# Softmax over 32,768 columns on one Trainium2 core: part of two stores cut into transfers of a few partitions

## Chip, core and metric

One core of a Trainium2 chip runs the kernel. The metric is device time in microseconds (us), the median of several runs; less is better. Besides the compute engines, the core has 16 DMA engines, which carry out all transfers between the chip's main memory (HBM) and its on-chip memory (SBUF, 128 partitions). A transfer is issued by one of the engines SP, ACT or GpSimd (POOL), each through its own queue, and ends by raising a semaphore by 16, on which others wait.

## What is computed

```python
logits = np.random.randn(16, 256, 32768).astype(np.float32)   # temperature = 1.0
scaled = logits / temperature
scaled = scaled - scaled.max(axis=-1, keepdims=True)
exp_scaled = np.exp(scaled)
return exp_scaled / exp_scaled.sum(axis=-1, keepdims=True)
```

A softmax over each of 4096 rows of 32,768 float32: 537 MB are read and as many written.

## The kernel before

Each row is cut in two halves of 16,384 columns, so that there are 8192 half rows; 128 of them, one per partition, make a chunk, and there are G = 64 chunks. Two neighbouring partitions hold the halves of one row. A chunk is handled in two column pieces (c = 0 and 1) of `_CW` = 8192 columns, 32 KB per partition and 4 MB in all. SBUF holds six such pieces, the slots of the tensor `xs` (`X` in the code); chunk g uses slots 2g mod 6 and the next, so three chunks are in work at a time.

For a chunk, VectorE takes the maximum of each piece (L123), ScalarE (ACT) replaces the piece by its exponentials and sums them (L168), VectorE combines the pieces and the two halves of each row by a few operations on 128 x 4 numbers (L134 to L153), and then scales both pieces (L157). Results lie in the slots where the logits were. The scaling of piece k raises the semaphore `sc` k of its chunk, for which the store waits.

The order of each queue is written out by hand:

- SP issues the loads. The first chunk's two pieces are loaded in two transfers of 4096 columns each (`load_edge`, L98), the next two chunks' whole (`load`, L90). Then a loop of 20 turns loads three chunks per turn: for each of the six slots it waits until the slot's last store has landed (`st[b]`) and issues the load. After the loop come the loads of the last chunk, in four transfers.
- ACT issues the stores (`store`, L103) of chunks 0 to 60, each right behind its own work on that chunk: those of chunk 0 ahead of its loop, the others within it.
- SP issues the stores of the last three chunks, G-3, G-2 and G-1, after its loads: two transfers for each of the first two, four for G-1. At the end SP waits until every slot's stores have landed.
- GpSimd takes no part, but for four small memsets at the start.

`Half` is the class that holds the work of a chunk; its method `stores` waits for each piece's `sc` and issues its store. `first()`, `turn(q, i)` and `last(g)` make such objects for chunk 0, for those of the loop and for the last three. The semaphores `ld` and `st` have one for each slot, and are never set back: a wait asks for 16 times the number of transfers so far.

## Time and profile before

| | |
|---|---|
| median of 3 runs | 2488.28 us (2488.11 to 2488.37) |
| the profiled execution | 2488.27 us, its span 2486.5 us |
| moved | 1073.77 MB, 432 GB/s over the span |
| VectorE busy | 1724.6 us (69%) |
| ScalarE busy | 944.5 us (38%) |
| GpSimd busy | 0.2 us, 4 instructions |
| a load of 4 MB | 26.5 us from issue to landing (median) |
| a store of 4 MB by ACT | 48.3 us from issue to landing (median) |
| a store of 4 MB by SP | 33.7 us from issue to landing (median) |

The span runs from the first instruction to the last. The profile's page divides it into 40 slices; in the row of the DMA engines, a digit is the mean busy share of all 16 in tenths, 9 for 90% and more. Queue q1 holds the transfers that SP issues, q10 those of ACT, q14 the fetches of instructions. In a timeline, a line begins with the start and the time taken, then the engine (SPq and ACTq are the parts of SP and ACT that issue transfers), the line of the kernel, the operation and what it writes from what. In the table of windows the columns are named in its first line. The trace also has a record of every packet of the DMA engines (start, time taken, size, queue, but not the engine) and of each of the 16 raises of a transfer's semaphore, its landings.

### The profile page before, as it was taken

To read this page: it belongs to the slowest core of one execution; us is meant where nothing else is said; L and a number is where in the kernel's file an instruction comes from. 1 tells how busy PE (TensorE), PEld (TensorE's weight loads), DVE (VectorE), ACT (ScalarE), POOL (GpSimd) and SP (SyncE) were. 2 spreads that over 40 slices of the span, in tenths; PEclk is the share of its full clock that TensorE was granted. 3 is DMA by queue.
4 is the path that set the end of the run, shared out by engine and by line. 5 is a ranking of instruction groups with operands and counts; after the bars stand their busy time and mean duration, and the time that the engine had idled before them with its cause. 6 is when DMAs were issued, how large, how long until landed. Compare 5 with 4: busy or idle time off the path is not lost.

```text
span 2486.5 us, 2019 instructions
## 1 busy us (share of the span) xinstructions
DVE 1724.6 (69%) x644; ACT 944.5 (38%) x325; POOL 0.2 (0%) x4
## 2 busy tenths in 40 slices
DVE  6777767767677676676766767667676676766764
ACT  3444333343333433434334343343433434334342
POOL 0000000000000000000000000000000000000000
DMA  9999999999999999999999999999999999999999
GB/s 413 430 435 433 430 438 431 430 438 431 432 436 431 436 432 431 438 430 432 437 430 434 435 430 438 431 430 438 431 432 436 431 436 432 431 438 431 430 437 399
DMA packets 37730, 1073.77 MB, mean 432 GB/s; under 512 B 4192, under 2 KB 4192, under 8 KB 4192
## 3 DMA queue, kind: packets, MB, share of 16 engines
q1 hardware_dynamic: 20160, 562.05, 52.4%
q10 hardware_dynamic: 17568, 511.71, 47.7%
q14 instruction: 2, 0.02, 0.0%
HBM read 536.87 MB, written 536.87 MB: 432 GB/s over the span
## 4 chain that ended last, share of the span: by engine, by line
DMA 58%; DVE 18%; another core or an unknown queue 14%; ACT 8%; issue 1%; SPq 0%; ACTq 0%; DVEq 0%
DMA out_dram<-xs 37%; DMA xs<-in_logits_dram 21%; DVE t L123 11%; ACT xs L168 7%; DVE xs L157 6%; SPq L90 0%; ACT ee L179 0%; DVE t L134 0%; DVE row L153 0%; DVE row L138 0%; DVE junk L142 0%; ACTq L103 0%; SPq L98 0%; DVEq L133 0%
## 5 line engine op out<-in xcount | busy, mean ns | idle before, releaser
L168 ACT ACTIVATE xs<-xs,t 128x8192 f32<-128x8192 f32 (+1 forms) x130 | 912.1, 7016 | 1468.4 <-DVE t L123 1468.4
L123 DVE TENSOR_REDUCE t<-xs 128x1 f32<-128x8192 f32 (+1 forms) x130 | 1110.8, 8551 | 234.0 <-DMA xs<-in_logits_dram 234.0
L157 DVE TENSOR_SCALAR xs<-xs,ee,row 128x8192 f32<-128x8192 f32 (+1 forms) x130 | 576.5, 4478 | 2.3
L134 DVE LOAD_MASK_SELECT t<-t x64 | 0.9, 14 | 470.3 <-ACT xs L168 470.3
L179 ACT ACTIVATE ee<-t,row 128x4 f32<-128x4 f32 x64 | 19.0, 298 | 35.9 <-DVE row L138 35.9
L142 DVE CUSTOM_DVE_ANT_1 junk<-ee,t 128x4 f32<-128x4 f32 x64 | 10.4, 163 | 23.3 <-ACT ee L179 23.3
L168 ACT ACTIVATION_READ_ACCUMULATOR xs<-xs,t 128x1 f32 x130 | 24.3, 187 | 0.0
L153 DVE RECIPROCAL row<-row 128x1 f32<-128x1 f32 x64 | 10.5, 164 | 2.2
L138 DVE TENSOR_REDUCE row<-t 128x1 f32<-128x4 f32 x64 | 10.1, 157 | 2.2
L134 DVE STREAM_SHUFFLE t<-t 128x4 f32<-128x4 f32 x64 | 10.2, 160 | 0.6
L142 DVE DVE_READ_ACCUMULATOR2_ANT row<- 128x1 f32 x64 | 5.3, 82 | 0.0
L168 ACT ACT_TABLE_LOAD x1 | 1.3, 1283 | 0.9 <-SPq L54 0.9
L272 POOL MEMSET const-bfloat16-1.0<- 128x1 bf16 x1 | 0.1, 102 | 0.0
L272 POOL MEMSET const-uint8-127<- 128x1 uint8 x1 | 0.1, 101 | 0.0
L272 POOL MEMSET const-float32-0.0<- 128x1 f32 x1 | 0.1, 99 | 0.2 <-issue 0.2
L272 POOL MEMSET const-float32-1.0<- 128x1 f32 x1 | 0.1, 98 | 0.0
## 6 DMA issues: line engine op xcount, KB each, us to landing
xs<-in_logits_dram SPq DMA_DIRECT2D x124, 4096.0 KB, 26.5
out_dram<-xs ACTq DMA_DIRECT2D x122, 4096.0 KB, 48.3
xs<-in_logits_dram SPq DMA_DIRECT2D x8, 2048.0 KB, 16.1
out_dram<-xs SPq DMA_DIRECT2D x4, 4096.0 KB, 33.7
out_dram<-xs SPq DMA_DIRECT2D x4, 2048.0 KB, 21.9
```

Source lines behind the costliest of these rows:

```text
L123: m = dve.tensor_reduce(out=t[:, k : k + 1], in_=xcols(self.slots[c], s, w), axis=X_, op=A.max, negate=True)
L134: dve.stream_shuffle(out=t[:, 2 * K : 4 * K], in_=t[:, 0 : 2 * K], mask=swap).then_inc(site(tag, "sh"), 1)
L138: dve.tensor_reduce(out=r[:, 0:1], in_=tv[:, :, 0, :], axis=XY, op=A.min).then_inc(site(tag, "mx"), 1)
L142: dve.tensor_tensor_reduce(out=j[:, 0 : 2 * K].rearrange("p (a k) -> p a k", a=2), in0=e[:, 0 : 2 * K].rearrange("p (a k) -> p a k", a=2), ...
L153: dve.reciprocal(out=r[:, 2:3], in_=r[:, 1:2]).then_inc(site(tag, "rc"), 1)
L157: dve.tensor_scalar(out=xs, in0=xs, scalar1=e[:, k : k + 1], scalar2=r[:, 2:3], op0=A.mult, op1=A.mult).then_inc(site(tag, "sc", k), 1)
L168: a = act.activation(out=xs, in_=xs, func=Exp, bias=t[:, k : k + 1], scale=inv_t, accum_out=t[:, K + k : K + k + 1],)
L179: act.activation(out=e[:, 0 : 2 * K].rearrange("p (a k) -> p a k", a=2), in_=tv[:, :, 0, :], func=Exp, bias=r[:, 0:1], scale=-1.0,).then_i ...
L272: nc = _bacc.Bacc("TRN2", target_bir_lowering=False, num_devices=1)
```

## The change

Two stores are cut.

Chunk 0, first piece: ACT stores the first 6144 of its 8192 columns as before. The last 2048 columns are stored by GpSimd, which waits for the same semaphore, in transfers of 15 partitions: eight of them, and a ninth of 8. They raise a semaphore `pool` of their own. SP waits for all nine after the first six pieces are loaded, ahead of its loop, since the loop's first load overwrites that slot.

Chunk G-2 (62 of 0 to 63), first piece: SP stores the first 6400 columns as before. The last 1792 follow in 29 transfers, issued by SP one after the other: 7, 6, 5, 4, 3, 2 and 1 partitions, four times over, which makes 112 partitions, and one of 16. They raise a semaphore `stair`, for which SP waits at the end. The chunk's second piece is stored after them.

```diff
+_TURNCOLS = 2048
+_STAIRCOLS = 1792
...
+    n_pool = -(-P // 15)
+    sp.wait_ge(site("pool"), 16 * n_pool)
     with sp.Fori(1, turns + 1) as i:
...
     f = first()
     f.scalar()
-    f.stores(act, 0)
+    cut = _CW - _TURNCOLS
+    act.wait_ge(site(f.tag, "sc", 0), 1)
+    store(act, 0, 0, 0, 0, cut)
+    act.wait_ge(site(f.tag, "sc", 1), 1)
+    store(act, 0, 1, 1, 0, _CW)
+
+    pool = nc.gpsimd
+    pool.wait_ge(site(f.tag, "sc", 0), 1)
+    for p in range(0, P, 15):
+        n = min(15, P - p)
+        pool.dma_start(out=o[bass.ds(p, n), cut:_CW], in_=X[p : p + n, cut:_CW]).then_inc(site("pool"), 16)
...
+    n_stair = 0
     for g in range(G - 3, G):
-        last(g).stores(sp, g)
+        h = last(g)
+        if g != G - 2:
+            h.stores(sp, g)
+            continue
+
+        b, keep = h.slots[0], _CW - _STAIRCOLS
+        sp.wait_ge(site(h.tag, "sc", 0), 1)
+        store(sp, g, 0, b, 0, keep)
+        p = 0
+        while p < P:
+            for n in [7, 6, 5, 4, 3, 2, 1] if p < 112 else [16]:
+                sp.dma_start(
+                    out=o[bass.ds(g * P + p, n), keep:_CW],
+                    in_=X[p : p + n, b * _CW + keep : (b + 1) * _CW],
+                ).then_inc(site("stair"), 16)
+                n_stair += 1
+                p += n
+        sp.wait_ge(site(h.tag, "sc", 1), 1)
+        store(sp, g, 1, h.slots[1], 0, _CW)
+    sp.wait_ge(site("stair"), 16 * n_stair)
```

## Prediction

> **What bounds the kernel now.** I read the slices of the span first, then the queues, the windows at the end, and last the timelines of the first stores and the last transfers.

> ```profile
> DVE 1724.6 (69%) x644; ACT 944.5 (38%) x325; POOL 0.2 (0%) x4
> ...
> DMA  9999999999999999999999999999999999999999
> ...
> q1 hardware_dynamic: 20160, 562.05, 52.4%
> q10 hardware_dynamic: 17568, 511.71, 47.7%
> ```

> No slice has the 16 DMA engines under nine tenths, and the two queues (q1 issued by SP, q10 by ACT) add up to 100% of 16 engines' span, while VectorE has 31% to spare. A 128-row DMA makes 144 packets: 128 rows and 16 of 4 bytes that raise the semaphore. So q10's 122 stores have 15,616 rows in 47.7% of 16 x 2486.5 us: 1.215 us for a row of 32 KB. The packet records agree: median 1.213 us for 32 KB, 0.611 for 16 KB, 0.009 for 4 bytes. Counted over time they show 16 packets in flight from 2 us to 2482 us, one per engine, with no hole. So this is sixteen servers that never rest. A change matters only by (a) work added to an engine, (b) an engine left without work, (c) how evenly they finish.

> ```profile
> core 0: us, DVE busy (x) ACT busy (x) POOL busy (x), PEclk, DMA share, GB/s
> 2446.00:2482.00 36.00, 10.06 (x10) 3.17 (x3) 0.00 (x0) 1.00 0.99 424
> 2482.00:2486.00 4.00, 0.00 (x0) 0.00 (x0) 0.00 (x0) 1.00 0.07 29
> ```

> The DMA share falls from 0.99 to 0.07: the engines do not stop together. In the packet records 13 stop by 2482.40, three at 2482.85, 2483.41 and 2484.85. One engine is 2.45 us late, and that sets the end. It drifts: the 16 semaphore landings of a store lie 0.31 us apart at 230 us, 0.51 at 463, 2.33 at 2089 and 2.82 at 2485. Which engine it is the trace does not name.

> ```profile
> 0.95 1.91 SPq L98 DMA_DIRECT2D xs<-in_logits_dram  x4
> ...
> 44.70 4.80 ACTq L103 DMA_DIRECT2D out_dram<-xs  x2
> ...
> 79.60 4.77 ACTq L103 DMA_DIRECT2D out_dram<-xs  x2
> ...
> 118.52 17.27 DVE L123 TENSOR_REDUCE t<-xs 128x1 f32<-128x8192 f32 x2
> ```

> Four issues by SP take 1.91 us, so one costs SP 0.48. The first chunk's stores are issued at 44.70 and 49.15. The first slot's landed at 68.40, and SP reloaded that slot at 68.59; its data are first read at 118.52.

> ```profile
> 2423.30 4.79 SPq L103 DMA_DIRECT2D out_dram<-xs  x2
> 2452.62 7.30 SPq L103 DMA_DIRECT2D out_dram<-xs  x4
> ```

> These are the last six stores: chunk G-2 at 2423.30 and 2427.76, the last chunk from 2452.62. But they are moved much later: the landings of G-3's two stores are at 2436.76 and 2446.47, of G-2's at 2456.19 and 2465.87. The queue is some 20 us deep here.

> **The change, part by part.** No byte is added. The question is which engine moves it, and at what rate.

> *First chunk.* The last 2048 of 8192 columns (8 KB per row) leave ACT's first store and go out by nine GpSimd DMAs: eight of 15 rows and one of 8. ACT's store issues are unchanged in number. SP waits for all nine before its loop. Queued behind that wait is the reload of slot 0, then all later loads; who waits for it is VectorE's reduction at 118.52. If the nine are issued as fast as SP issues (0.48 each: 4.3 us), eight small packets per engine take turns with a load and a store packet, 8 x (2 x 1.213 + 0.31) = 22 us, so they land near 70 us instead of 68.40. Meanwhile the engines have the load that landed at 75.67, the store that landed at 87.43, and the stores issued at 79.60 and 84.02, each 9.7 us of work at full rate: work to about 100 us. So the delay of the load costs nothing unless GpSimd needs over (100 - 45)/9 = 6.1 us for a transfer. The added semaphore packets are 8 or 9 x 0.009 = 0.1 us.

> The row's tail cost 8/32 of 1.213 = 0.303 us. What does it cost as a packet of its own? There is no 8 KB store in the trace. The nearest rows are the 8 KB instruction fetches of q14: 0.309 us when alone (2355 and 2383 us), 0.474 and 0.531 when two overlapped, 0.493 to 0.568 when three did, before the span. [...] I take 0.568: 8 x (0.568 + 0.009 - 0.303) = +2.2 us on every engine. Bounds: 0.309 gives +0.1; four abreast in line (4 x 0.309) gives +7.5; an engine that gets no row gains 2.4.

> *Late chunk.* G-2's first store loses its last 1792 columns (7 KB per row) to 29 SP DMAs: four cycles of 7, 6, 5, 4, 3, 2, 1 rows, then one of 16. SP needs 28 to 29 x 0.48 = 14 us more, so G-2's second store is issued near 2437.5 instead of 2427.76. The engines reach it only after about 2454 (2446.47 and the shortened first store), so this is hidden; the cover ends at 1.1 us per issue. SP's queue held the 8 first loads (over 60 packets per engine) without blocking, so the depth is no matter either.

> What is not hidden is the share-out. A transfer of n rows, n under 8, cannot use 16 engines by whole rows. Either each starts at the same engine, or they are dealt on in turn. In the trace every DMA gives each engine the same eight rows, as far as 16 equal shares can tell, so nothing decides. I take the fixed start, as it needs no memory from one DMA to the next. Then the first engine gets one row of each of the 29, the second 25, the third 21, down to 5 on the seventh and 1 on the last nine; before, each had 8. For the first engine, the tails cost 8 x 0.265 = 2.12 us before. Now a packet costs 7/8 of an 8 KB one: 0.270 to 0.497. At 0.497: 29 x (0.497 + 0.009) - 2.12 = +12.55 us; at 0.270, +5.97; at four abreast, +29.5; dealt in turn, 8 x 0.279 - 2.12 = +0.1. Behind these packets stand G-2's second store and the last chunk's four, each shared by all engines, so nothing can even it out before the end. [...]

> [...]

> *Sum.* Late engine replaced as the last: -2.45, if it is not among the first two. 2.2 + 12.55 - 2.45 = **+12.3 us**. The profiled span of 2486.5 becomes 2498.8; what lies around it was 1.8 us (that execution took 2488.27, the median is 2488.28), so **2500.6 us**.

> **Rivals.** (0.2%, 5.0 us, is about what a measurement tells from no change.)

> 1. *Skew without slowing.* Small packets run at full rate: 0.1 + 5.97 - 2.45 = +3.6, **2491.9**. For it: 16 KB packets cost half of 32 KB ones to within 0.009 us. [...] If the late engine is the first, +6.1.
> [...]
> 3. *Not slower.* The rows are dealt out in turn, at full rate: 0.1 + 0.1, **2488.5**; if the 15-row transfers also pass over the late engine, 2.4 less, 2486.1. It decides as long as no engine gets more than 2.45/0.279 = 9 rows too many, for then the late engine still ends last. Against: it needs an even deal on SP's queue, with 28 starts.
> 4. *GpSimd is late.* At 8 us per transfer the nine land at 117; the engines run dry from 100 for 17 us: 17 + 3.6 = +20.6, **2509**. For it: GpSimd does only four memsets before, so nothing prices its transfers. Against: 6.1 us each are covered.

> **Chances.** Forecast 0.42, rivals 1 to 4: 0.18, 0.25, 0.09, 0.06. Slower by over 0.2% (above 2493.3): forecast, 2 and 4, and the worse end of 1: 0.74. Within: the rest of 1 and 3: 0.24. Faster: even all of the late engine's 2.45 us is 0.1%, so 0.02. The range runs from below rival 1 (2490) to above rivals 2 and 4 (2511); left out are rival 3 and the four-abreast bound of the stair.

> **What would show it.** Skew: in the last windows the DMA share falls over some 15 us, not 3, and the landings of the last stores lie that far apart. Even deal: they stay 3 us apart. Slowing: 7 and 8 KB packets take 0.5 us, not 0.3, and between 45 and 75 us the GB/s drop. GpSimd late: the reload of slot 0 is issued after 100 us, and the slices near 100 us lose their nines. Wrong altogether: an end that moves with neither.

## The result, and the profile after

The changed kernel took 2507.08 us in the median of nine runs, against 2488.28 us before. Over the runs that the comparison keeps, the ratio is 1.0046 (95% interval 1.0033 to 1.0060), some 11 us. The nine runs are the first surprise: 2496.4, 2496.6, 2499.5, 2501.8, 2507.1, 2540.0, 2669.5, 2708.7 and 2742.5, where nine runs of the kernel before lay between 2488.0 and 2492.3. The comparison leaves out runs over 1.5% above a kernel's fastest, but they are taken here as part of what the change does, since none of the 88 runs of the kernel before, over this and the comparisons below, took more than 2492.4 us.

The profiled execution is the one of 2507.08 us, with a span of 2505.3. From its page, the engines, the slices and the queues:

```profile
DVE 1724.9 (69%) x644; ACT 944.5 (38%) x325; POOL 8.5 (0%) x13
...
DMA  9999999999999999999999999999999999999998
GB/s 406 418 434 434 432 432 433 433 431 430 428 429 426 430 433 429 430 432 433 432 434 432 433 433 433 432 433 433 432 433 433 432 433 433 433 433 433 432 425 345
...
q1 hardware_dynamic: 20416, 562.05, 52.3%
q10 hardware_dynamic: 17568, 510.66, 47.4%
q0 software_dynamic: 288, 1.05, 0.2%
```

The new queue, q0 (GpSimd's), holds next to nothing. The engines are busy in all slices but the last, so nothing starved. Yet they moved less in some: 426 to 430 GB/s in the tenth to fourteenth slices, some 560 to 880 us into the run, where nothing of the change is under way. There the packets took longer: 184 of the 4107 of 32 KB that started from 563 to 877 us took over 1.275 us, up to 2.213, where none did in before. The last windows of the same kernel, columns as before:

```profile
2446.00:2482.00 36.00, 27.10 (x14) 15.50 (x9) 0.00 (x0) 1.00 0.99 407
2482.00:2486.00 4.00, 0.00 (x0) 0.00 (x0) 0.00 (x0) 1.00 1.00 426
2486.00:2494.00 8.00, 0.00 (x0) 0.00 (x0) 0.00 (x0) 1.00 0.87 371
2494.00:2503.00 9.00, 0.00 (x0) 0.00 (x0) 0.00 (x0) 1.00 0.19 80
```

Where the share fell from 0.99 to 0.07 within one window before, it is now 0.87 from 2486 us and still 0.19 from 2494: the engines finish far apart. The 16 landings of the last store lie 10.7 us apart (2492.3 to 2503.0), where they lay 2.8 apart before. The timelines of GpSimd, VectorE and SP near the first store:

```profile
45.01 8.32 POOL L254 DMA_DIRECT2D out_dram<-xs  x9 [44.56 <-DVE xs L159]
```

```profile
40.16 9.00 DVE L159 TENSOR_SCALAR xs<-xs,ee,row 128x8192 f32<-128x8192 f32 x2
```

```profile
85.53 34.83 SPq L92 DMA_DIRECT2D xs<-in_logits_dram  x4
```

GpSimd needs 8.32 us for its nine issues, but SP's first reload goes out at 85.53 us, not at 68.59 as before, nor near 70 as forecast.

Two readings of the trace's packet records are used below. *Lost time* at t is the bytes moved by t in the kernel before, less those of the kernel in question, over 16 engines at 27.0 GB/s (32 KB in 1.213 us, the median of before): how far the engines are behind on the average. *Spread* is the time from the first to the last of the 16 landings of one 128-row transfer, load or store. Engines are *in step* as long as it is small.

### The profile page after: what moved, and what is told of

Same layout as the page of the kernel before. It is cut to its first block, busy times and chain, and to the rows that moved or that the text cites. A ratio compares the mean times of both kernels' runs of the same rounds, so it can differ in the third digit from the quotient of the medians.

```text
span 2505.3 us, 2060 instructions
## 1 busy us (share of the span) xinstructions
DVE 1724.9 (69%) x644; ACT 944.5 (38%) x325; POOL 8.5 (0%) x13
## 2 busy tenths in 40 slices
DMA packets 38275, 1073.78 MB, mean 429 GB/s; under 512 B 4480, under 2 KB 4480, under 8 KB 4608
## 3 DMA queue, kind: packets, MB, share of 16 engines
q1 hardware_dynamic: 20416, 562.05, 52.3%
q10 hardware_dynamic: 17568, 510.66, 47.4%
## 4 chain that ended last, share of the span: by engine, by line
DMA 61%; DVE 25%; ACT 9%; another core or an unknown queue 2%; issue 2%; POOL 0%; SPq 0%; DVEq 0%; ACTq 0%
DMA xs<-in_logits_dram 32%; DMA out_dram<-xs 29%; DVE t L125 15%; DVE xs L159 9%; ACT xs L170 9%; ACT ee L181 0%; POOL out_dram L254 0%; DVE t L136 0%; DVE row L155 0%; DVE row L140 0%; DVE junk L144 0%; SPq L92 0%; SPq L100 0%; ACTq L105 0%
## 5 line engine op out<-in xcount | busy, mean ns | idle before, releaser
L254 POOL DMA_DIRECT2D out_dram<-xs x9 | 8.3, 933 | 44.6 <-DVE xs L159 44.6
```

Of the source, the lines that this page charges most:

```text
L254: pool.dma_start(out=o[bass.ds(p, n), cut:_CW], in_=X[p : p + n, cut:_CW]).then_inc(site("pool"), 16)
```

## The experiments

Theory A is the prediction's: a price where the small transfers stand, nothing in between. Theory B came from the trace of after: the first transfers throw the engines out of step, and engines out of step slow each other to the end. Medians, and the ratio to the kernel before on the same chip:

```
kernel             median    lowest..highest  runs  ratio (95% interval)
turn_only          2507.71   2497.8..2718.6     6   1.0056 (1.0040..1.0072)
stair_only         2495.46   2495.0..2496.2     6   1.0030 (1.0018..1.0041)
turn_one128        2488.22   2487.7..2488.9    11   1.0000 (0.9991..1.0009)
drain              2501.44   2501.3..2503.1     5   1.0054 (1.0041..1.0067)
turn8_near         2498.76   2497.7..2778.5     9   1.0058 (1.0034..1.0082)
turn8_far          2492.66   2490.4..2614.8    12   1.0022 (1.0012..1.0033)
stair_even16       2489.43   2489.2..2489.8    11   1.0005 (0.9996..1.0013)
late15             2490.10   2489.4..2495.0    11   1.0009 (1.0000..1.0017)
late_reload        2490.43   2489.2..2655.3    12   1.0008 (0.9999..1.0017)
turn_nowait        2493.92   2491.1..2502.8     8   1.0028 (1.0018..1.0039)
turn8_far_nowait   2518.26   2497.9..2550.6     6   1.0143 (1.0104..1.0183)
turn16_nowait      2495.37   2491.3..2499.2     7   1.0024 (1.0013..1.0035)
```

And the lost time of an engine, in us, with the median spread between 300 and 1000 us:

```
time t             110    300    1000   2300   2450   spread
before              0      0      0      0      0      0.75
after               2.9    2.9    7.5    9.5   10.6    4.4
turn_only           2.9    3.8    8.7   11.0   13.9    9.8
stair_only         -0.1    0      0      0      0      0.7
turn_one128         0.1    0.1    0.1    0.1    0.1    0.7
drain               6.1    6.1    6.1    6.1    6.1    0.7
turn8_far           2.3    2.5    2.5    2.5    2.5    1.5
late_reload         2.3    2.3    2.3    2.3    2.3    2.7
turn_nowait         1.8    2.2    2.2    2.2    3.4    6.6
turn8_far_nowait    0.5    0.8    0.9    5.1    7.5    5.8
turn16_nowait       1.6    2.5    3.1    3.2    5.8    5.1
```

The intervals of stair_even16, late15 and late_reload reach 1, so by them alone these three are no slower. But none of their 34 runs is as fast as the slowest of before beside them (2488.8 and 2488.9 us), so the 1 to 2 us are taken as real.

The trace of turn8_near is of one of its long runs, 2778.5 us, and shows what such a run loses: 5.0 us by 110 us, 88 by 1000 and 235 by 2300. Two of its windows:

```profile
300.00:1000.00 700.00, 427.60 (x160) 235.60 (x80) 0.00 (x0) 1.00 0.94 385
1000.00:2300.00 1300.00, 808.45 (x300) 434.59 (x149) 0.00 (x0) 1.00 0.93 384
```

Here the DMA share is down as well. Of the 230 us lost between 110 and 2300 us, 95 are packets of 32 KB that took longer than 1.213 us, and 135 are engines without work. Between 2000 and 2300 us, 15 of the 16 landings of a store lie within 2.3 us, and the last comes 19.8 to 32.1 us after the first: one engine has fallen far behind, and the others wait for it.

**turn_only**: the stair undone.

```diff
     for g in range(G - 3, G):
-        h = last(g)
...
-    sp.wait_ge(site("stair"), 16 * n_stair)
+        last(g).stores(sp, g)
```

> Chunk 0's tail by GpSimd in 15-row transfers alone, the stair undone. Theory A (as predicted: a price at the place of the small transfers, nothing in between): +2 to +3 us, 2490 to 2491, all runs within 1 us. Theory B (the 15-row transfers throw the 16 engines out of step, and for the rest of the run packets now and then take longer than 1.213 us, as 409 of the 32 KB ones did between 300 and 2300 us in the profile of after): +6 us or more, 2494 to 2700, runs tens of us apart, and a landing spread of over 4 us through the run.

2507.71 us, the runs 121 us apart in all: theory B's numbers, not A's. The second table shows it too: 2.9 us are lost by 110 us, and 8 more between 110 and 2300 us. In these 2200 us, 702 packets of 32 KB took more than 1.275 us, against none in before. In after, what the packets of 32 KB took beyond 1.213 us in these 2200 us comes to 6.7 us per engine, and 6.6 us were lost: in these two runs the loss is long packets, and no engine stood idle. (The count of 409 for after in the expectation is wrong: between 300 and 2300 us it is 514.) The two parts of the change do not simply add: turn_only alone is as slow as both together, as its cost differs by tens of us from run to run.

**stair_only**: chunk 0's store whole again, with no GpSimd and no wait for it.

```diff
-    sp.wait_ge(site("pool"), 16 * n_pool)
...
-    cut = _CW - _TURNCOLS
...
-        pool.dma_start(out=o[bass.ds(p, n), cut:_CW], in_=X[p : p + n, cut:_CW]).then_inc(site("pool"), 16)
+    f.stores(act, 0)
```

> The stair alone, chunk 0's store whole again. Theory A: skew of the first engine by 29 small packets, slowed: +6 to +10 us, 2494 to 2498; at full rate +3.6, plus 1.2 us for the instruction fetch that SP has at the end of the changed program: 2493. Theory B: the same price as A at full rate, 2491 to 2494, and the runs agree within 1 us, since the engines are in step until 2450 us. If rows were dealt out in turn: 2488.5 to 2490.

2495.46 us, +7.3 us, six runs within 1.3 us. The price is the one of theory A with slowed packets; theory B's, at most 2494, was too low, but nothing is lost until 2450 us, as it had it. Then it is skew: some engines get more of the work than others and finish later. In the windows of this run:

```profile
2446.00:2482.00 36.00, 10.06 (x10) 2.98 (x3) 0.00 (x0) 1.00 0.99 409
2482.00:2486.00 4.00, 0.00 (x0) 0.00 (x0) 0.00 (x0) 1.00 0.33 139
2486.00:2494.00 8.00, 0.00 (x0) 0.00 (x0) 0.00 (x0) 1.00 0.10 42
```

The mean share of the engines is a third after 2482 us and a tenth after 2486. The 16 landings of the last store lie in two groups, nine between 2481.9 and 2483.4 and seven between 2486.4 and 2491.6. How the rows were dealt out shows in the 128 packets of 7 KB: they run from 2450.8 to 2462.1 us, and from 2459 us on no more than two are under way at a time. One engine with 29 of them would need 29 x (0.349 + 0.009) = 10.4 us, at the mean that they took; an even deal, eight each, would be over in some 3. So a few engines got most of them, as a fixed start has it. The groups of nine and seven do not show it by themselves: G-2's second store lands in eleven and five. Which engine is the late one of before stays open. It landed G-2's first store at 2454.03, and eight rows and one small packet take 9.9 us at least (8 x 1.213 + 0.272 = 10.0; the landings of before lie 9.65 apart), so it can't have landed G-2's second store before 2463.9: it is one of the last five, from 2467.3 on. The instruction fetch that I had expected to add 1.2 us was there (2492.6 us), but the time from the last packet to the end grew by 0.4 only.

**turn_one128**: no stair, and GpSimd's nine transfers as one of 128 rows, for which SP waits.

```diff
-    for p in range(0, P, 15):
-        n = min(15, P - p)
+    for p in range(0, P, P):
+        n = P
```

> Chunk 0's tail by GpSimd in one transfer of 128 rows, no stair. If the third queue itself throws the engines out of step: as turn_only (theory B: 2494 or more, runs far apart). If it is the transfers of 15 neighbouring rows: engines stay within 1 us of one another and the time is 2488 to 2489.

2488.22 us, equal to before, runs within 1.2 us, all 128 packets of 8 KB at 0.309 us. GpSimd's queue as such costs nothing, nor does cutting the store, nor a first reload at 73.8 us instead of 68.6.

**drain**: the whole change, but the queues run empty once after the nine.

```diff
     sp.wait_ge(site("pool"), 16 * n_pool)
+    for b in range(2):
+        sp.wait_ge(st[b], 16)
+    for b in range(2, _BUFS):
+        sp.wait_ge(ld[b], 16)
...
+    drained = [(site("pool"), 16 * n_pool), (st[0], 16), (st[1], 16)] + [(ld[b], 16) for b in range(2, _BUFS)]
...
             h.scalar()
+            if q == 0:
+                for sem, v in drained:
+                    act.wait_ge(sem, v)
             h.stores(act, i * _SETS + (q + 1 - _SETS))
```

> The whole change, and SP's first reload and ACT's store of chunk 1 wait until every transfer so far has landed (near 85 us), so that all 16 engines start again together; the empty queues cost 3 to 6 us once. Theory A: that much more than after, 2505 to 2512, or at best the same. Theory B: the runs no longer lie apart (within 2 us), the landing spread between 150 and 2300 us is back to some 0.5 to 3 us, no long packets there, and the time is stair_only plus 5 to 9 us: 2497 to 2503.

This run decides between A and B. The windows of drain, then those of after, over the same four stretches, and one of before:

```profile
44.00:110.00 66.00, 50.23 (x21) 29.45 (x10) 8.33 (x9) 1.00 0.95 389
110.00:300.00 190.00, 134.63 (x51) 73.63 (x25) 0.00 (x0) 1.00 1.00 433
300.00:1000.00 700.00, 487.34 (x181) 265.07 (x90) 0.00 (x0) 1.00 1.00 434
1000.00:2300.00 1300.00, 905.85 (x334) 491.24 (x166) 0.00 (x0) 1.00 1.00 433
```

```profile
44.00:110.00 66.00, 50.23 (x21) 29.45 (x10) 8.32 (x9) 1.00 1.00 408
110.00:300.00 190.00, 133.72 (x44) 72.56 (x23) 0.00 (x0) 1.00 1.00 434
300.00:1000.00 700.00, 485.06 (x180) 259.22 (x91) 0.00 (x0) 1.00 1.00 430
1000.00:2300.00 1300.00, 904.10 (x339) 492.84 (x168) 0.00 (x0) 1.00 1.00 433
```

```profile
300.00:1000.00 700.00, 487.26 (x181) 265.08 (x90) 0.00 (x0) 1.00 1.00 434
```

The drain shows as a DMA share of 0.95 and 389 GB/s near the start: 6.1 us lost instead of 2.9. From there it is the kernel before again: 434 GB/s and not 430 between 300 and 1000 us, no 32 KB packet over 1.275 us between 110 and 2300, a spread of 0.7 us. Five runs lie within 1.8 us. The sum closes: 6.1 us at the start and stair_only's +7.3 make 13.4; measured was 2501.44 - 2488.19 = 13.25 (the profiled run is 1.6 us above that median). Some 3 us more at the start (6.1 against 2.9) buy off the 6.6 us that after lost between 110 and 2300 us in its profiled run, and the differences between runs. It is not a gain on every run: its ratio of 1.0054 is no better than the 1.0046 of after, and three of after's nine runs were below 2500. What goes is the runs of 2540 to 2743 us.

Next, what throws the engines out of step. Theory N: neighbouring rows read at once. Theory U: the uneven share of 15 rows.

**turn8_near** and **turn8_far**: no stair, 16 transfers of 8 rows, once neighbours, once 4 rows apart.

```diff
-    for p in range(0, P, 15):
-        n = min(15, P - p)
+    for p in range(0, P, 8):
+        n = 8
```

```diff
-    for p in range(0, P, 15):
-        n = min(15, P - p)
-        pool.dma_start(out=o[bass.ds(p, n), cut:_CW], in_=X[p : p + n, cut:_CW])
+    for q in range(P // 8):
+        p = 64 * (q % 2) + 32 * (q // 2 % 2) + q // 4
+        pool.dma_start(out=o[p : p + 29 : 4, cut:_CW], in_=X[p : p + 29 : 4, cut:_CW])
```

> No stair; chunk 0's tail by GpSimd in 16 transfers of 8 neighbouring rows (0 to 7, 8 to 15, ...). Theory N (neighbouring rows read at once by several engines wait for each other, and that throws the engines out of step): small packets over 0.309 us as in turn_only, lost time through the run, 2494 to 2700, runs apart. Theory U (it is the uneven share of 15 rows, one engine left out of each transfer): 8 rows on 8 engines by turns stay as even as may be, so in step: 2488 to 2490.

> As turn8_near, but each of the 16 transfers takes 8 rows 4 apart (0, 4, ..., 28, then 64, 68, ..., 92, and so on). Number and size of the transfers are the same. Theory N: small packets all near 0.309 us, landing spread under 3 us, 2488 to 2490 and runs within 1 us. Theory U, or any cost of many small GpSimd transfers: the same as turn8_near, whatever that is.

On the small packets the two differ as theory N has it: with neighbours, 22 of 128 took over 0.400 us, up to 1.352; 4 rows apart, all took 0.309 to 0.325. On the time, N was only half right: far is 6 us better in the median, but 4 us worse than before, and two of its 12 runs were at 2507.5 and 2614.8. Something else disturbs. (The expectation took it that 8-row transfers would go to 8 engines by turns. In turn8_far_nowait, below, they did not; if so here as well, both kernels had an uneven share, and theory U was not tested.)

**stair_even16** and **late15**: no turn; the stair's tail in eight transfers of 16 rows, or 2048 columns in eight of 15 rows and one of 8.

```diff
-            for n in [7, 6, 5, 4, 3, 2, 1] if p < 112 else [16]:
+            for n in [16]:
```

```diff
-_STAIRCOLS = 1792
+_STAIRCOLS = 2048
...
-            for n in [7, 6, 5, 4, 3, 2, 1] if p < 112 else [16]:
+            for n in [min(15, P - p)]:
```

> No turn; chunk G-2's tail of 1792 columns by SP in eight transfers of 16 rows in place of the 29. Skew theory (the first engines get most of the 29): an even share takes the skew away, landings of the last stores 3 to 5 us apart again, and only the slowing of neighbouring rows at the end is left: +1 to +2.5 us, 2489 to 2491. If the cost of the stair were its 14 us of SP's issues or slowed packets rather than skew: 2493 or more.

> No turn; chunk G-2's tail of 2048 columns by SP in eight transfers of 15 rows and one of 8. If SP's small transfers always start at the same engine, the 16th gets none of the 128 rows and is done 2.4 us earlier. If the engine that is 2.45 us late in before is that one: 2486.5 to 2489 (less 2.4, plus 1 to 2.5 for neighbouring rows). If it is another engine: 2490 to 2492. If the rows are dealt out in turn: as stair_even16.

In transfers of 16 rows, the same tail costs +1.1 us and not +7.3. Its windows have no work left after 2486 us:

```profile
2482.00:2486.00 4.00, 0.00 (x0) 0.00 (x0) 0.00 (x0) 1.00 0.42 180
2486.00:2494.00 8.00, 0.00 (x0) 0.00 (x0) 0.00 (x0) 1.00 0.00 0
```

Its small packets are over after 5.8 us, not 11.3. So some 6.2 of the stair's 7.3 us are skew, and the rest fits slowed packets: they took 0.408 us in the mean, 0.272 at full rate, which for eight on an engine makes 8 x 0.136 = 1.1. late15, +1.8 us, came out at the lower edge of its case that another engine than the late one is left out. Its landings fit that: the first of G-2's second store came at 2462.53, while the two latest engines had landed the store before at 2453.43 and 2453.80 and need 9.65 us for eight rows. So the first was neither of these two. Nor can it have had eight tails, which even at full rate would have put it past 2463. An engine on time and with none would at full rate have landed by 2461.4; so full packets were slowed as well.

**late_reload**: the kernel before, with SP's first reload held back, and nothing else.

```diff
+    sp.wait_ge(st[1], 16)
     with sp.Fori(1, turns + 1) as i:
```

> The kernel before, with one wait more: SP's first reload waits for the store of slot 1 as well, so it is issued at some 82 us or later and not at 68.6, as in turn_only (87.2). Nothing is sent by GpSimd. Theory W (the late reload throws the engines out of step): 2490 to 2500, runs more than 2 us apart, landing spread above the 0.3 to 2.8 us of before. Theory N (only neighbouring rows do): 2488.0 to 2489.0, runs within 1 us, spread as in before.

**turn_nowait** and **turn8_far_nowait**: turn_only and turn8_far with the tail copied aside by ScalarE, so that the reload needn't wait for GpSimd's transfers.

```diff
+    spare = nc.alloc_sbuf_tensor("spare", [P, _TURNCOLS], fp32)
...
-    sp.wait_ge(site("pool"), 16 * n_pool)
     with sp.Fori(1, turns + 1) as i:
...
     act.wait_ge(site(f.tag, "sc", 0), 1)
+    act.activation(out=spare[:, :], in_=X[:, cut:_CW], func=mybir.ActivationFunctionType.Copy).then_inc(site("copied"), 1)
+    act.wait_ge(site("copied"), 1)
...
-    pool.wait_ge(site(f.tag, "sc", 0), 1)
+    pool.wait_ge(site("copied"), 1)
...
-        pool.dma_start(out=o[bass.ds(p, n), cut:_CW], in_=X[p : p + n, cut:_CW])
+        pool.dma_start(out=o[bass.ds(p, n), cut:_CW], in_=spare[p : p + n, :])
...
+    sp.wait_ge(site("pool"), 16 * n_pool)
     total = [0] * _BUFS
```

> turn_only with the tail copied by ScalarE to a place of its own first, and sent from there by GpSimd in the same 15-row transfers, so that SP's first reload doesn't wait for them (issue near 68 us). Theory N: out of step all the same, 2491 or more, runs tens of us apart. Theory W: 2488.5 to 2491 and runs within 1 us (the slowed small packets cost 1 to 2 us where they stand).

> turn8_far (rows 4 apart) with the same copy and no wait of SP's. If what was left of turn8_far's cost (2.5 us between 75 and 100 us, two of its 12 runs 15 and 122 us up) is the late reload: 2488 to 2489, runs within 1 us. If it is the many small GpSimd transfers: as turn8_far, 2490 to 2494 and now and then far above.

The late reload alone costs +2.1 us: 2.2 us are lost between 80 and 100 us, once, with 47 packets of 32 KB over 1.275 us, up to 2.465, and the spread goes to 2.7 us; one run of 12 was at 2655, the others within 2.0 us. So theory W is right that a late reload disturbs. But taking it away cures neither kernel: turn_nowait +5.6 us, and turn8_far_nowait, whose small packets all take 0.309 us, is the worst of all at +29.9 us. My expectation for it, 2488 to 2489, failed. Its packet records tell why the engines part: the first transfers' small packets start in bursts of eight at 53.7, 58.3, 62.8 and 67.4 us, though GpSimd issues the transfers 0.52 us apart. If the second went to the other eight engines, it would start near 54.2. So eight engines get all 16 small packets and the others none, 16 x 0.309 = 4.9 us of difference. turn8_far has the same transfers, yet a spread of only 1.5 us. It sent its first reload at 90.5 us, and its engines were short of work by 4% between 70 and 90 us, so it may have lined up again as in drain; this was not tried.

**turn16_nowait**: turn_nowait with eight transfers of 16 rows.

```diff
-    for p in range(0, P, 15):
-        n = min(15, P - p)
+    for p in range(0, P, 16):
+        n = 16
```

> turn_nowait with eight GpSimd transfers of 16 neighbouring rows in place of the nine: every engine gets eight small packets, where in turn_nowait and turn8_far_nowait the packet records show the transfers coming one behind the other on the same 15 or 8 engines (bursts of 15 or 8 packets some 4 us apart, none of another engine in between). Theory U (the uneven share throws the engines out of step): 2488.5 to 2490, runs within 1 us. Theory N (neighbouring rows are enough): small packets of up to 1.4 us as before, 2491 or more, runs several us apart.

2495.37 us, runs 8 us apart: with 16 rows to a transfer and no wait of SP's, neighbouring rows are enough as well (26 of 128 small packets over 0.400 us, up to 2.206, and a spread of 5.1 us). A caveat for all three kernels with the copy: their first two reloads still went out at 69.7 to 70.9 and 90.3 to 92.6 us, against 68.6 and 87.9, and a kernel with the copy alone was not run. So neither N, U nor W is the one cause: the 16 engines part with slowed packets (turn16_nowait, a spread of 5.1 us), with an uneven share (turn8_far_nowait, 5.8 us) and with a late reload (late_reload, 2.7 us), and runs that lie apart follow in every case (for the late reload, in one run of 12). One transfer of 128 rows (turn_one128, 0.7 us) does not part them, and a drain (0.7 us) undoes it. Being apart is not itself a price, though: turn_nowait lost nothing between 300 and 2300 us, with spreads up to 10.9 us, and paid again at 2410 to 2430 us, behind the last loads.

## Why the prediction came out as it did

The forecast was 2500.6 us, range 2490 to 2511; measured was 2507.08 us. The sign and the size are right, but one term of the sum was missing, and another too large. By the ratio of 1.0046 the change takes 2499.7 us, and the forecast lies closer still; but with runs from 2496 to 2743 us a hit within 1 us is luck.

- *"A change matters only by (a) work added to an engine, (b) an engine left without work, (c) how evenly they finish"*: this step failed. There is a (d): once the engines have parted, a packet can take longer. That cost 6.6 us between 110 and 2300 us in the profiled run (9.5 - 2.9), and 8 us in turn_only's. A row of 32 KB took 1.213 us in before, and I took that for the engine's price; it was the price at a spread of 0.75 us, and at 4.4 us, in after, 515 rows took over 1.275 us in these 2200 us. In the long run of turn8_near the prediction's own (b) comes on top: 135 of the 230 us are engines without work, most of them in the end waiting for one that is some 20 us or more behind.
- *GpSimd's transfers, +2.2 us on every engine*: 2.9 us were lost by 110 us, but by another mix. The small packets took 0.461 us in the mean, not 0.568 (an estimate, from three fetches that overlapped), which makes 8 x (0.461 + 0.009 - 0.303) = +1.3 us. That every engine gets eight of them no run shows: the first 15 started from 54.51 to 54.80 us, the next 15 from 57.87 to 59.38, by the look of it on the same engines. The late reload, priced at nothing, costs 2.1 us when tried alone.
- *"They land near 70 us"*: the nine landed by 85.2, since a transfer's packets waited about 4 us behind those of the one before, not 2.74. The cover to 100 us did hold, in that the engines had work (DMA share 1.00 from 44 to 110 us); the reload still wasn't free: in late_reload, packets of 32 KB took up to 2.465 us behind it.
- *The stair, 12.55 - 2.45 = +10.1 us*: +7.3 us alone. The share-out fits the fixed start that was assumed (11.3 us of small packets, against 5.8 in stair_even16), with skew the main part (some 6.2 us). The size of the packet was off: 0.349 us in the mean in stair_only, not 0.497 (7/8 of that 0.568). With it, 29 x (0.349 + 0.009) - 2.12 = +8.3 us for the first engine; the last landing was 8.8 us behind the thirteenth of before (2491.57 against 2482.75). The prediction took off 2.45 us on the condition that the late engine is not among the first two; the runs do not say which it is.
- *Four abreast in line, +7.5 us at the start and +29.5 in the stair*: no run shows such a line of four. Neighbouring rows did slow small packets, up to 1.352 us in turn8_near against at most 0.325 in turn8_far; but in the mean they took 0.461 us in after and 0.349 in stair_only, where four in line would make 1.236 (4 x 0.309) and 1.080 (4 x 0.270).
- *14 us of SP's issues, hidden*: right. The 29 issues moved G-2's second store by over 11 us, and nothing is lost before 2450 us in stair_only. They took 16.1 us in all: the first 26 took 0.3 to 0.4 us each, the last two 2.4 and 2.3. What held those two no run shows, so it stays open whether the queue's depth is no matter:

```profile
2423.49 16.08 SPq L263 DMA_DIRECT2D out_dram<-xs  x29
2439.61 20.12 SPq L105 DMA_DIRECT2D out_dram<-xs  x5
```

- *Rivals.* The skew without slowing (2491.9) is too low even for stair_only. An even deal, at 2488.5, is not what SP's queue did (11.3 us of small packets in stair_only); with 16 rows to a transfer, in stair_even16, the time is 2489.4. That the measured time lies so near the forecast is in part two errors that cancel: 2.8 us too much for the stair (10.1 against 7.3), 6.6 us forgotten in between.

Open is why packets take longer once the engines have parted, and why some offsets do it and others not. In after, 514 packets of 32 KB started between 300 and 2300 us and took over 1.275 us; among those that overlap in time, 387 pairs were two loads, 238 two stores and 17 mixed. So 625 of these 642 pairs are of one direction; where they meet was not tried. Nor is it settled why one run loses 8 us by it and another 250: the one long run with a trace shows an engine that falls over 20 us behind, but not why.

## What to carry to other kernels

Where all DMA engines are busy throughout, as here, what counts is not bytes but the slowest engine: the bytes stayed the same (1073.78 MB against 1073.77), and the 16 landings of the last store lay 10.7 us apart instead of 2.8. Send a piece in one 128-row transfer: the first chunk's tail cost nothing that way (2488.22 us). The late chunk's cost +1.1 us in 16-row transfers and +7.3 in a staircase. Do not disturb the engines early in a long stream, as the loss can go on (2.9 us by 110 us in after, 9.5 by 2300); if a ragged transfer is needed there, let the queues run empty once behind it, which cost some 3 us here and did away with the long runs (five within 1.8 us). And where a kernel's runs lay within 1 us of one another, runs tens of us apart are themselves the finding.
